# Into the MLP: order of the late operand sums, where the upper squares are summed, and which engine splits the last output weights

## The chip, the cores and the metric

One core of a Trainium2 chip runs the whole program in one launch. The metric is the time on the device in microseconds (us). All numbers are 32-bit floats. TensorE multiplies, VectorE and ScalarE and GpSimd work element by element, and the queues that SyncE issues move data to and from device memory.

## The reference, cut to what matters

Two layers of a decoder trunk on 1040 tokens (16 learned ones and 1024 given ones) of width 1024. Layer 0 mixes by a short convolution and a gated delta rule, layer 1 by windowed attention; each layer then has a gated MLP. What lies around the change is the end of each mixer and the beginning of each MLP:

```python
h = h + mix                                  # mix = heads @ w_out (or wo)
hn = h * rsqrt(mean(h*h, -1) + EPS) * w      # rms_norm, per token
gate, val = split(hn @ w_up, 2)              # 1024 -> 2 x 2816
gate = causal_dwconv(gate, conv_w)           # width 3
h = h + (silu(gate) * val) @ w_down
```

## The kernel before, in words

Activations stand with the model dimension on the 128 partitions: `h` is eight tiles `h[0]` to `h[7]` of 128 by 1040 tokens. Each product of full precision is made of three reduced ones: every operand x is split into a high part (a cast by ScalarE) and a low part (x minus the high part, by VectorE, or by GpSimd in `load_w`), and TensorE adds high*high, high*low and low*high.

The up projection (`ffn`) takes its product of a 2 by 2 block matrix (weights: gate and value, lower and upper half of the model dimension; tokens: lower and upper half, `tk[0]` and `tk[1]`, of 520 tokens each in layer 0 and 516 in layer 1) with seven block products instead of eight. There are 22 columns of blocks i, and each makes products 0 to 6. Their token operands are X[0] to X[6], made once per layer by `parts` (L747): X[0] and X[1] are the lower tokens of either half of the model dimension times the norm's weight, X[2] and X[3] are sums of blocks (L783 to L788), X[4], X[5] and X[6] are the late ones: sums by L792 and L795, and one plain block. Each X[j] has four tiles k, and each tile costs one cast on ScalarE and one subtraction on VectorE (L751, or L754 with the norm's weight). The weights' operands are sums as well: `w1` is the gate's weights themselves, `w2` is split from `sa` (L869, L870), `w3` and `w4` from `sb` (L879, L887) and a raw block, each split by `wsplit` (L809 cast, L810 low part).

The products run in two accumulators of PSUM, `A` and `C`, of two buffers each. In block i, `A` holds products 0, 2, 4 and 5 one after the other, and ScalarE copies it out between them (`snap`, L826: `p1` after product 0, `u2` after product 2, `u3` after product 4); product 1 has a `C` of its own, and products 3 and 6 share one. So product 4 can't start before the copy `u2` is made. The first product of block i+1 is issued inside block i.

The norm's factor is one number per token, so it is applied late, on the results (L896). Its making stands between the early and the late operands in the program: for each half s of the tokens, ScalarE squares `h[k]` (L737, L740), VectorE adds the eight squares into `ss[s]` (L741), TensorE sums over the partitions with a matrix of ones (L760, into a `C`), and a chain of steps between ScalarE (L763, L764, L766) and VectorE (L767, L768, twice) makes the inverse root. Both halves share the scratch tiles `sg`, `th` and `u2`, so the second half's chain follows the first's, and the copy `u2` of block 0 follows both.

The order of instructions on an engine is not the order of the text. A planner, run when the program is built, plays the program on a clock of its own and lists for each engine what is ready, in the main the earlier line first; `tc.issue_after(ins)` makes it list every instruction of a block that runs on `ins`'s engine behind `ins`. On the chip each engine keeps that list's order. The tiles of X beyond the first five take the places of the mixer's result tiles, which come free as TensorE reads them for the last time.

The mixer of layer 0 ends with eight output products (L692 to L699, in the order h0, h4, h1, h5, h2, h6, h3, h7). That of layer 1 ends with `outputs(1, yb, QCH[2:])` (L1229): four weights, each loaded by `load_w` (L129; the low part by GpSimd at L135), and for each two short products of the last 346 tokens, added to `h` at L1205.

Of the kernel before, what the change touches and what calls it, by code (L numbers as in the profile page):

```python
# [7 lines left out]
F32 = mybir.dt.float32  # L8
# [3 lines left out]
AF = mybir.ActivationFunctionType  # L12
ALU = mybir.AluOpType
# [5 lines left out]
KT = D // P  # L19
# [63 lines left out]
def trunk(tc, hT0, w_in, w_ab, w_out, w_q, w_k, w_v, w_o, w_up, w_down, vec, cst, out):  # L83
# [3 lines left out]
    with ctx:  # L87
# [40 lines left out]

        def load_w(src, nk, name):  # L129
            raw = wp.tile([P, nk, P], F32, tag="wraw", name=name + "r")  # L130
            sp.dma_start(raw, src)
            hi = wp.tile([P, nk, P], F32R, tag="whi", name=name + "h")
            lo = wp.tile([P, nk, P], F32R, tag="wlo", name=name + "l")
            ac.copy(hi, raw)  # L134
            gp.tensor_tensor(lo, raw, hi.bitcast(F32), ALU.subtract)  # L135
            return hi, lo
# [569 lines left out]
        def ffn(h, layer, last):  # L706
# [10 lines left out]
            with tc.tile_pool(name=f"fx{layer}", bufs=5, side="right", reuse_waits="tile") as xb:  # L717
                with tc.tile_pool(name=f"f{layer}", bufs=1, reuse_waits="tile") as fp, \
# [11 lines left out]

                    sums = full("r", 2)
                    ss = [sums[:, s * hf:s * hf + hf] for s in range(2)]
                    for j, k in enumerate((0, 4, 1, 5, 2, 6, 3, 7)):
                        sp.dma_start(hd[k][:, o0:], h[k][:, o0:])
                        for s in range(2):
                            if j == 0:
                                ac.activation(ss[s], h[k][:, tk[s]], AF.Square)  # L737
                            else:
                                sq = half("p1", 1, "sq") if s else half("u3", 1, "sq")
                                ac.activation(sq, h[k][:, tk[s]], AF.Square)  # L740
                                ve.tensor_tensor(ss[s], ss[s], sq, ALU.add)  # L741

                    X = [[None] * 4 for _ in range(7)]

                    def parts(j, k, src, vcol=None):
# [3 lines left out]
                        if vcol is None:  # L749
                            ac.copy(hi, src)  # L750
                            ve.tensor_tensor(lo, src, hi.bitcast(F32), ALU.subtract)  # L751
                        else:
                            ac.activation(hi, src, AF.Copy, scale=vcol)
                            ve.scalar_tensor_tensor(lo, src, vcol, hi.bitcast(F32), ALU.mult, ALU.subtract)  # L754
                        X[j][k] = (hi, lo)

                    def scales(s):
                        ps = wide("C")
                        for b in range(2):
                            pe.matmul(ps[:, b, :q], ones, ss[s][:, b * q:b * q + q], start=True, stop=True)  # L760
                        a, t = (x[:, :hf] for x in (full("sg"), full("th")))
# [25 lines left out]
                    for k in range(4):  # L787
                        parts(3, k, B(0, k, 0))  # L788
                    for s in range(2):
                        scales(s)  # L790
                    for k in range(4):
                        ve.scalar_tensor_tensor(B(0, k, 1), B(1, k, 1), w[4 + k], B(0, k, 1), ALU.mult, ALU.subtract)  # L792
                        parts(4, k, B(0, k, 1))
                    for k in range(4):
                        ve.scalar_tensor_tensor(B(1, k, 0), B(1, k, 0), w[4 + k], t2[k], ALU.mult, ALU.subtract)  # L795
                        parts(5, k, B(1, k, 0))
                        parts(6, k, B(1, k, 1), w[4 + k])

# [60 lines left out]
                    for i in range(NF):  # L859
# [8 lines left out]
                        sa = fp.tile([P, KT, P], F32, tag="ws", name="sa", bufs=2)  # L868
                        ve.tensor_tensor(sa[:, 4:8], v1, v2, ALU.add)  # L869
                        ve.tensor_tensor(sa[:, 0:4], sa[:, 4:8], g1, ALU.subtract)  # L870
                        w2 = wtile()
                        wsplit(w2, 0, KT, sa)
                        product(A, w2, 0, 2, False)
# [4 lines left out]
                        sb = fp.tile([P, KT, P], F32, tag="ws", name="sb", bufs=2)  # L878
                        ve.tensor_tensor(sb[:, 0:4], g1, v1, ALU.subtract)  # L879
                        w3 = wtile()  # L880
                        wsplit(w3, 0, 4, sb[:, 0:4])
                        wsplit(w3, 4, 4, v2)
                        product(A, w3, 0, 4, False)
                        u3 = snap("u3", A)
                        v = full("v")
                        ve.tensor_tensor(two(v[:, hf:2 * hf]), two(u3), C[:, :, :q], ALU.subtract)  # L886
                        ve.tensor_tensor(sb[:, 4:8], sa[:, 0:4], g2, ALU.subtract)  # L887
                        if i + 1 < NF:
# [3 lines left out]
                        w4 = wtile()  # L892
                        wsplit(w4, 0, 4, sb[:, 4:8])
                        product(C, w4, 0, 6, False)
# [42 lines left out]
        def swa(h, sqp):  # L937
# [5 lines left out]
            with tc.tile_pool(name="l1", bufs=1, reuse_waits="tile") as lp:  # L943
# [248 lines left out]

                def outputs(G, ys, cs, pairs=range(4)):
                    for i in pairs:
                        w = load_w(w_o[i, G], 8, "wo")
                        for j in range(2):
# [31 lines left out]
                parts(1, yb, QCH[2:])  # L1228
                outputs(1, yb, QCH[2:])  # L1229
            return ho[0::2] + ho[1::2]  # L1230
# [80 lines left out]
```

## Time and profile before

| | |
|---|---|
| median of 3 runs | 2427.57 us (2425.96 to 2429.2) |
| the profiled execution: its own time | 2428.64 us |
| the profiled execution: span from the first to the last instruction | 2426.9 us |
| TensorE matmul, busy | 2345.5 us, 97% |
| VectorE, busy | 1656.2 us, 68% |
| ScalarE, busy | 981.6 us, 40% |
| GpSimd, busy | 483.6 us, 20% |
| mean granted TensorE clock | 0.989 of full speed |

The span holds the mixer of layer 0 up to 583.7 us, its MLP up to about 1296 us, the mixer of layer 1 up to 1709.5 us and its MLP to the end. PE is TensorE's matmul, PEld its weight load, DVE is VectorE, ACT is ScalarE, POOL is GpSimd and SP is SyncE. In a timeline the matmuls overlap, so a matmul's cost to the stream is the distance to the start of the next one.

### The profile page before, as it was taken

The page shows a single profiled execution, that of the slowest core. Times are in us where ns is not written, and L with a number is a line of the kernel's source. Part 1 is how long each engine was busy: PE and PEld are TensorE (multiplying, and loading weights), DVE is VectorE, ACT ScalarE, POOL GpSimd, SP SyncE. Part 2 cuts the span into 40 slices and gives each one's busy share as a digit, 9 for nine tenths or more (in the row PEclk, how much of TensorE's full clock was granted, in tenths as well). Part 3 has the DMA queues.
Part 4 walks back from the last instruction along what each step waited for, and adds up shares of the span by engine and source line. Part 5 has one row for each costly group of instructions (what it writes and reads, how often), then busy time and mean ns, then how long its engine had stood idle before and what let it go on. Part 6 is the DMA issues. An engine that isn't in the chain of part 4 may idle for free.

```text
span 2426.9 us, 40063 instructions
## 1 busy us (share of the span) xinstructions
PE 2345.5 (97%) x16060; PEld 2214.8 (91%) x16060; DVE 1656.2 (68%) x2836; ACT 981.6 (40%) x1980; POOL 483.6 (20%) x421
## 2 busy tenths in 40 slices
PE   8999999999899999999999999999699999999999
PEld 7989999998899999999999987878699999998887
DVE  8886735667677777785536578778877777778432
ACT  6445213435344444432225456645544444433110
POOL 1113323520000000012225245454000000002221
PEclk9999999999999999999999999999899999999999
DMA  3234434141122222253212100202222222234222
GB/s 136 93 111 133 162 120 142 58 167 71 71 79 79 80 79 79 76 194 114 85 61 106 44 27 19 96 18 82 93 79 79 83 81 80 81 140 159 86 66 100
DMA packets 93481, 224.83 MB, mean 93 GB/s; under 512 B 18672, under 2 KB 30264, under 8 KB 93296
## 3 DMA queue, kind: packets, MB, share of 16 engines
q1 hardware_dynamic: 93296, 222.28, 26.7%
q8 instruction: 126, 2.06, 0.3%
q14 instruction: 59, 0.48, 0.1%
HBM read 166.08 MB, written 56.15 MB: 92 GB/s over the span
## 4 chain that ended last, share of the span: by engine, by line
PE 82%; DVE 12%; ACT 4%; issue 1%; DMA 1%; POOL 0%; SPq 0%; ACTq 0%; DVEq 0%; POOLq 0%
PE mm L147 38%; PE A L820 20%; PE C L820 15%; PE po L1020 1%; DVE qt L251 1%; PE scp L1074 1%; DVE yl L171 1%; ACT sc L1092 1%; DVE X L751 1%; PE qkp L973 0%; ACT xh L182 0%; PE po L1143 0%; DVE Xd L499 0%; DVE wlo L810 0%; DVE fq L497 0%
## 5 line engine op out<-in xcount | busy, mean ns | idle before, releaser
L820 PE MATMUL A<-X,whi 128*128 128x260 f32 (+1 forms) x2816 | 515.3, 284 | 16.4 <-ACT u L826 15.8
L147 PE MATMUL mm<-y,wdh 128*128 128x346 f32 (+2 forms) x1760 | 471.1, 350 | 1.6 <-DVE r L895 1.6
L820 PEld LDWEIGHTS A<-X,whi 128*128 128x128 f32 x2816 | 436.1, 190 | 17.9 <-ACT u L826 17.0
L820 PE MATMUL C<-X,whi 128*128 128x260 f32 (+1 forms) x2112 | 391.5, 284 | 7.7 <-DVE v L886 5.9
L820 PE MATMUL A<-X,wlo 128*128 128x260 f32 (+1 forms) x1408 | 394.2, 283 | 0.0
L135 POOL TENSOR_TENSOR wdl<-wdr,wdh 128x512 fp32r<-128x512 f32 (+1 forms) x80 | 117.8, 1473 | 1301.4 <-ACT wdh L134 1297.0
L147 PEld LDWEIGHTS mm<-y,wdh 128*128 128x128 f32 x1760 | 315.1, 188 | 32.8 <-DVE r L895 2.1
L820 PEld LDWEIGHTS C<-X,whi 128*128 128x128 f32 x2112 | 329.2, 190 | 8.6 <-DVE v L886 6.3
L147 PE MATMUL mm<-y,wdl 128*128 128x346 f32 (+2 forms) x880 | 307.4, 350 | 0.0
L820 PE MATMUL C<-X,wlo 128*128 128x260 f32 (+1 forms) x1056 | 297.2, 283 | 0.0
L820 PEld LDWEIGHTS A<-X,wlo 128*128 128x128 f32 x1408 | 265.6, 190 | 0.0
L931 DVE TENSOR_TENSOR h<-mm,h 128x346 f32<-128x346 f32 (+2 forms) x200 | 115.9, 583 | 208.0 <-PE mm L147 207.5
L820 PEld LDWEIGHTS C<-X,wlo 128*128 128x128 f32 x1056 | 200.0, 190 | 0.0
L147 PEld LDWEIGHTS mm<-y,wdl 128*128 128x128 f32 x880 | 165.5, 188 | 15.4
L810 DVE TENSOR_TENSOR wlo<-sa,whi 128x1024 fp32r<-128x1024 f32 x44 | 53.9, 1225 | 171.4 <-ACT whi L809 171.4
L134 ACT CAST wdh<-wdr 128x512 fp32r<-128x512 f32 (+1 forms) x80 | 53.1, 664 | 265.5 <-PE mm L147 221.1
L809 ACT CAST whi<-sb 128x512 fp32r<-128x512 f32 x88 | 54.6, 621 | 130.2 <-PE C L820 128.4
L147 PE MATMUL mm<-xl,wqkvh 128*128 128x346 f32 (+1 forms) x288 | 96.0, 333 | 1.3 <-DVE xl L183 1.3
L826 ACT COPY u<-A 128x520 f32<-128x520 f32 (+1 forms) x88 | 52.1, 592 | 111.4 <-PE A L820 108.3
L147 PE MATMUL mm<-xh,wqkvh 128*128 128x346 f32 (+1 forms) x288 | 96.2, 337 | 0.7 <-DVE row L269 0.7
L809 ACT CAST whi<-sa 128x1024 fp32r<-128x1024 f32 x44 | 46.1, 1048 | 120.4 <-PE A L820 120.4
L147 PE MATMUL mm<-xh,wqkvl 128*128 128x346 f32 (+1 forms) x288 | 93.3, 326 | 0.0
(401 smaller groups left out, 5259.1 us busy)
## 6 DMA issues: line engine op xcount, KB each, us to landing
wg<-in_w_up SPq DMA_DIRECT2D x44, 512.0 KB, 3.4
wv<-in_w_up SPq DMA_DIRECT2D x44, 512.0 KB, 3.4
wdr<-in_w_down SPq DMA_DIRECT2D x48, 256.0 KB, 2.6
fy<-sg SPq DMA_DIRECT2D x22, 520.0 KB, 2.6
yf<-fy SPq DMA_DIRECT2D x22, 520.0 KB, 4.9
fy<-sg SPq DMA_DIRECT2D x22, 516.0 KB, 2.6
yf<-fy SPq DMA_DIRECT2D x22, 516.0 KB, 4.7
wdr<-in_w_down SPq DMA_DIRECT2D x32, 320.0 KB, 3.0
```

Source lines behind the costliest of these rows:

```text
L134: ac.copy(hi, raw)
L135: gp.tensor_tensor(lo, raw, hi.bitcast(F32), ALU.subtract)
L147: pe.matmul(ps[:, :n], a[:, j, :], b[:, c0:c0 + n], start=(i == 0), stop=(i == last))
L171: ve.tensor_tensor(dst_l, src, dst_h.bitcast(F32), ALU.subtract)
L251: ve.scalar_tensor_tensor(d, buf[:, pad + c0 - i:pad + c0 - i + n], taps[W - 1 - i], tmp[:, :n], ALU.mult, ALU.add)
L751: ve.tensor_tensor(lo, src, hi.bitcast(F32), ALU.subtract)
L809: ac.copy(hi, src)
L810: ve.tensor_tensor(lo, src, hi.bitcast(F32), ALU.subtract)
L820: pe.matmul(ps[:, b, :q], a[:, at + k, :], x[:, c], start=(start and n == 0), stop=(n == 11), skip_group_check=not start)
L826: ac.copy(two(t), ps[:, :, :q])
L931: ve.tensor_tensor(hn[m][:, s], ps[:, :n], hn[m][:, s], ALU.add)
L1020: pe.matmul(ps, a, b, start=(start and j == 0), stop=(stop and j == 2))
```

## The change

There are four edits.

1. The squares of the upper tokens (s = 1) are no longer added by VectorE. TensorE multiplies each by the matrix of ones and adds them in a `C` named `upper`, taken at the beginning of `ffn`; each square is two matmuls more, and the upper half's own pair after the sum goes. The squares use the tiles `u2` and `p1` in turn.
2. The late operand sums (L792, L795) and the low parts of X[4], X[5] and X[6] are listed on VectorE behind `half_x`, the low part of the last tile of X[3].
3. The weight sums and splits of `w2` in block 1, and of `w3` and `w4` in blocks 0 and 1, are listed on VectorE behind `half_x` as well; the sum `sb[:, 4:8]` stands some lines earlier.
4. In layer 1's last output products, the weights' low part is made by VectorE and not by GpSimd.

```diff
-        def load_w(src, nk, name):
+        def load_w(src, nk, name, eng=gp):
...
-            gp.tensor_tensor(lo, raw, hi.bitcast(F32), ALU.subtract)
+            eng.tensor_tensor(lo, raw, hi.bitcast(F32), ALU.subtract)
...
-                    sums = full("r", 2)
-                    ss = [sums[:, s * hf:s * hf + hf] for s in range(2)]
+                    ss = full("r", 2)[:, :hf]
+
+                    upper = wide("C")
                     for j, k in enumerate((0, 4, 1, 5, 2, 6, 3, 7)):
                         sp.dma_start(hd[k][:, o0:], h[k][:, o0:])
-                        for s in range(2):
-                            if j == 0:
-                                ac.activation(ss[s], h[k][:, tk[s]], AF.Square)
-                            else:
-                                sq = half("p1", 1, "sq") if s else half("u3", 1, "sq")
-                                ac.activation(sq, h[k][:, tk[s]], AF.Square)
-                                ve.tensor_tensor(ss[s], ss[s], sq, ALU.add)
+                        if j == 0:
+                            ac.activation(ss, h[k][:, tk[0]], AF.Square)
+                        else:
+                            sq = half("u3", 1, "sq")
+                            ac.activation(sq, h[k][:, tk[0]], AF.Square)
+                            ve.tensor_tensor(ss, ss, sq, ALU.add)
+                        sq = half("u2" if j % 2 else "p1", 1, "sq")
+                        ac.activation(sq, h[k][:, tk[1]], AF.Square)
+                        for b in range(2):
+                            pe.matmul(upper[:, b, :q], ones, sq[:, b * q:b * q + q], start=(j == 0), stop=(j == 7))
...
                             ac.copy(hi, src)
-                            ve.tensor_tensor(lo, src, hi.bitcast(F32), ALU.subtract)
+                            last_lo[:] = [ve.tensor_tensor(lo, src, hi.bitcast(F32), ALU.subtract).ins]
...
                     def scales(s):
-                        ps = wide("C")
-                        for b in range(2):
-                            pe.matmul(ps[:, b, :q], ones, ss[s][:, b * q:b * q + q], start=True, stop=True)
+                        ps = upper
+                        if s == 0:
+                            ps = wide("C")
+                            for b in range(2):
+                                pe.matmul(ps[:, b, :q], ones, ss[:, b * q:b * q + q], start=True, stop=True)
...
                         parts(3, k, B(0, k, 0))
+
+                    half_x = last_lo[0]
                     for s in range(2):
                         scales(s)
-                    for k in range(4):
...
+                    with tc.issue_after(half_x):
+                        for k in range(4):
+                            ve.scalar_tensor_tensor(B(0, k, 1), B(1, k, 1), w[4 + k], B(0, k, 1), ALU.mult, ALU.subtract)
+                            parts(4, k, B(0, k, 1))
+                        for k in range(4):
+                            ve.scalar_tensor_tensor(B(1, k, 0), B(1, k, 0), w[4 + k], t2[k], ALU.mult, ALU.subtract)
+                            parts(5, k, B(1, k, 0))
+                            parts(6, k, B(1, k, 1), w[4 + k])
...
-                        ve.tensor_tensor(sa[:, 4:8], v1, v2, ALU.add)
-                        ve.tensor_tensor(sa[:, 0:4], sa[:, 4:8], g1, ALU.subtract)
                         w2 = wtile()
-                        wsplit(w2, 0, KT, sa)
+                        with tc.issue_after(half_x) if i == 1 else nullcontext():
+                            ve.tensor_tensor(sa[:, 4:8], v1, v2, ALU.add)
+                            ve.tensor_tensor(sa[:, 0:4], sa[:, 4:8], g1, ALU.subtract)
+                            wsplit(w2, 0, KT, sa)
...
-                        ve.tensor_tensor(sb[:, 0:4], g1, v1, ALU.subtract)
                         w3 = wtile()
-                        wsplit(w3, 0, 4, sb[:, 0:4])
-                        wsplit(w3, 4, 4, v2)
+                        with tc.issue_after(half_x) if i < 2 else nullcontext():
+                            ve.tensor_tensor(sb[:, 0:4], g1, v1, ALU.subtract)
+                            ve.tensor_tensor(sb[:, 4:8], sa[:, 0:4], g2, ALU.subtract)
+                            wsplit(w3, 0, 4, sb[:, 0:4])
+                            wsplit(w3, 4, 4, v2)
...
-                        ve.tensor_tensor(sb[:, 4:8], sa[:, 0:4], g2, ALU.subtract)
...
-                            wsplit(w4, 0, 4, sb[:, 4:8])
+                        with tc.issue_after(half_x) if i < 2 else nullcontext():
+                            wsplit(w4, 0, 4, sb[:, 4:8])
...
-                outputs(1, yb, QCH[2:])
+                outputs(1, yb, QCH[2:], eng=ve)
```

## Rows read from the trace of the kernel before

**Rows 1.** Busy time, share of the span and instructions of each engine (page).
```profile
PE 2345.5 (97%) x16060; PEld 2214.8 (91%) x16060; DVE 1656.2 (68%) x2836; ACT 981.6 (40%) x1980; POOL 483.6 (20%) x421
```

**Rows 2.** Stretches: length; busy (count) of PE, PEld, DVE, ACT, POOL; clock; DMA.
```profile
503.28:580.26 76.98, 76.98 (x484) 76.98 (x485) 44.06 (x58) 21.67 (x31) 14.36 (x6) 1.00 0.39 149
583.74:614.84 31.10, 20.10 (x154) 19.06 (x153) 29.62 (x48) 21.49 (x36) 0.00 (x0) 0.97 0.14 52
614.84:620.30 5.46, 5.45 (x24) 5.24 (x24) 0.00 (x0) 0.00 (x0) 0.00 (x0) 0.53 0.01 3
1689.54:1745.42 55.88, 36.75 (x227) 35.04 (x225) 54.57 (x82) 33.66 (x54) 5.31 (x2) 0.83 0.40 142
```

**Rows 3.** Chain that ended last, both entries: start, length, what.
```profile
613.40 0.71 DVE rstd L768
...
614.84 5.47 PE A L820 x24
...
1744.72 0.71 DVE rstd L768
...
1746.15 4.77 PE A L820 x24
```

**Rows 4.** Waits, 1680 to 1747 us: engine and line <- releaser: sum, times, longest.
```profile
PE C L760 <- DVE r L741: 7.9, 1, 7.9
...
PE A L820 <- ACT u L826: 7.2, 1, 7.2
PE mm L147 <- DVE h L1205: 6.5, 4, 2.8
PEld mm L147 <- issue: 5.5, 3, 3.1
```

**Rows 5.** Timeline of DVE, entry of layer 0: start, length, instruction.
```profile
562.11 2.90 DVE L792 SCALAR_TENSOR_TENSOR h<-h,vt,h 128x520 f32<-128x520 f32 x1
...
568.29 0.68 DVE L879 TENSOR_TENSOR sb<-wg,wv 128x512 f32<-128x512 f32 x1
...
589.76 0.69 DVE L741 TENSOR_TENSOR r<-r,sq 128x520 f32<-128x520 f32 x1
590.37 0.68 DVE L869 TENSOR_TENSOR sa<-wv 128x512 f32<-128x512 f32 x1
590.97 0.75 DVE L795 SCALAR_TENSOR_TENSOR h<-h,vt,v 128x520 f32<-128x520 f32 x1
591.64 0.69 DVE L767 TENSOR_TENSOR th<-sg,th 128x520 f32<-128x520 f32 x1
...
595.90 1.30 DVE L751 TENSOR_TENSOR X<-h,X 128x520 fp32r<-128x520 f32 x2
```

**Rows 6.** Timeline of DVE, entry of layer 1.
```profile
1692.79 2.47 DVE L741 TENSOR_TENSOR r<-r,sq 128x516 f32<-128x516 f32 x1 [0.57 <-ACT sq L740]
...
1695.61 0.68 DVE L741 TENSOR_TENSOR r<-r,sq 128x516 f32<-128x516 f32 x1
...
1698.58 2.86 DVE L792 SCALAR_TENSOR_TENSOR h<-h,vt,h 128x516 f32<-128x516 f32 x1
...
1719.85 0.69 DVE L767 TENSOR_TENSOR th<-sg,th 128x516 f32<-128x516 f32 x1
1720.45 0.69 DVE L741 TENSOR_TENSOR r<-r,sq 128x516 f32<-128x516 f32 x1
```

**Rows 7.** GpSimd's timeline there, and VectorE's split of 128x1024 (groups by form).
```profile
1692.30 2.40 POOL L135 TENSOR_TENSOR wol<-wor,woh 128x1024 fp32r<-128x1024 f32 x1 [2.77 <-ACT woh L134]
1697.97 2.91 POOL L135 TENSOR_TENSOR wol<-wor,woh 128x1024 fp32r<-128x1024 f32 x1 [3.27 <-PE mm L147]
...
L810 DVE TENSOR_TENSOR wlo<-sa,whi 128x1024 fp32r<-128x1024 f32 x44 | 53.9, 1225 | 171.4 <-ACT whi L809 171.4
```

**Rows 8.** Timeline of PE at the end of layer 0's mixer.
```profile
583.91 1.11 PE L760 MATMUL C<-r,ct 128*128 128x260 f32 x4 [0.17 <-DVE r L741]
584.67 0.59 PE L820 MATMUL A<-X,whi 128*128 128x260 f32 x2
```

More of the change, by code (lines that the diff above doesn't have):

```diff
@@ L1 @@
 import numpy as np
-from contextlib import ExitStack
+from contextlib import ExitStack, nullcontext
 import concourse.bass as bass
@@ L729, in full @@
                         return fp.tile([P, 2 + 2 * hf], F32, tag=tag, name=tag, bufs=bufs)
-                    sums = full("r", 2)
-                    ss = [sums[:, s * hf:s * hf + hf] for s in range(2)]
+                    ss = full("r", 2)[:, :hf]
+                    upper = wide("C")
                     for j, k in enumerate((0, 4, 1, 5, 2, 6, 3, 7)):
                         sp.dma_start(hd[k][:, o0:], h[k][:, o0:])
-                        for s in range(2):
-                            if j == 0:
-                                ac.activation(ss[s], h[k][:, tk[s]], AF.Square)
-                            else:
-                                sq = half("p1", 1, "sq") if s else half("u3", 1, "sq")
-                                ac.activation(sq, h[k][:, tk[s]], AF.Square)
-                                ve.tensor_tensor(ss[s], ss[s], sq, ALU.add)
+                        if j == 0:
[8 more added lines that the diff above has]
+                            pe.matmul(upper[:, b, :q], ones, sq[:, b * q:b * q + q], start=(j == 0), stop=(j == 7))
                     X = [[None] * 4 for _ in range(7)]
+                    last_lo = []
                     def parts(j, k, src, vcol=None):
@@ L788, in ffn @@
                         parts(3, k, B(0, k, 0))
+                    half_x = last_lo[0]
                     for s in range(2):
                         scales(s)
-                    for k in range(4):
[L792 to L797, printed above, removed]
+                    with tc.issue_after(half_x):
[6 more added lines that the diff above has]
+                            parts(6, k, B(1, k, 1), w[4 + k])
                     nw = [0]
@@ L1191, in parts, with outputs @@
                             split(ys[t][0][:, sl], ys[t][1][:, sl], qg[G][t][:, sl])
-                def outputs(G, ys, cs, pairs=range(4)):
+                def outputs(G, ys, cs, pairs=range(4), eng=gp):
                     for i in pairs:
-                        w = load_w(w_o[i, G], 8, "wo")
+                        w = load_w(w_o[i, G], 8, "wo", eng)
                         for j in range(2):
```

## The prediction

> **What bounds the kernel now.** The page first: TensorE is busy 97% of the span and VectorE 68% [rows 1], so only places where TensorE waits are worth anything. The stretches show two. At the end of layer 0's mixer TensorE has no hole at all (76.98 us busy of 76.98); then, entering the MLP, it is busy 20.1 us of 31.1 while VectorE is busy 29.6 of them. Entering layer 1's MLP it is 36.8 us of 55.9 against VectorE's 54.6, and the granted clock falls to 0.83 [rows 2]. So in both entries VectorE sets the pace. The chain says which of its work ends last: the second half's inverse root (L768, ending at 614.11 and at 1745.43 us), then the copy `u2`, then product 4 of block 0 [rows 3]. That product waits 7.2 us for the copy in layer 1, and before that product 1 stands 7.9 us behind the ones-matmuls that wait for the last sum of upper squares [rows 4]. Product 4 of layer 0, after its wait, runs at 0.53 of the clock, the lower of the two levels: 5.45 us for 24 matmuls [rows 2]. Until it, TensorE can do only products 0 to 3 of block 0 and 0 and 1 of block 1: the rest needs X[4] or a weight tile that is still in use. The time of an entry is therefore the time at which product 4 starts (with its four needs: X[4], the first half of `w3`, `u2`, and so the chain), plus what is put on TensorE before it.
>
> The order of VectorE is a plan's, and the diff changes only its rules. I count work that stands ahead of the chain's end before, and say what leaves and enters.
>
> **Prices.** A sum of 520 tokens costs VectorE 0.61 us (from L741 at 589.76 to the next start), a weight sum or split of 512 columns 0.60, a scaled sum (L792, L795, L754) 0.67 (590.97 to 591.64) [rows 5]; in layer 1 the same to 0.01. A split of 1024 columns costs 1.2 us [rows 7]. A pair of ones-matmuls holds TensorE 0.76 us, from 583.91 to the next matmul at 584.67 [rows 8].
>
> **Edit 1 in layer 0.** Of VectorE's seven additions for the upper tokens only the last (0.61 us, at 589.76) stands in the full stretch; the others stood where VectorE was busy 44 us of 77 [rows 2, 5] and are worth nothing. On TensorE eight pairs come. Seven squares are ready before the mixer's last matmul: 7 x 0.76 = 5.3 us, and with no hole in TensorE there, what is issued there costs in full. The plan could also hold them back into the entry, where TensorE waits anyway: 0. I take 5.3, the end that the full row shows. The eighth pair replaces the pair that goes.
>
> A rule of the Trainium skill weighs against this edit: "FP8 and Floating Point Precision", section "TensorE Precision Notes", has a true 32-bit product pass the array four times. By it a pair of 260 columns takes an estimated 2 x 4 x 260 / 2.4 GHz = 0.87 us, and seven pairs 6.1 us instead of 5.3, so that the gain below would be 0.8 us smaller. The trace shows 0.76 us [rows 8]; I go by that.
>
> **Edits 2 and 3 in layer 0.** What enters the full stretch: three L792 and one L795 that VectorE did before 580 us in idle time (the last L792 at 562.11), 4 x 0.67 = 2.7 us, and the two sums and two splits of `w3` of block 0, done from 568.29 on, 4 x 0.60 = 2.4 us [rows 5]. What can leave from ahead of the chain's end: the addition above, 0.6; block 1's two sums for `w2` (the first at 590.37), its two for `w3`, two splits and its L866, 7 x 0.60 = 4.2; the split of `w4`, 0.6. Sum: 2.7 + 2.4 - 0.6 - 4.2 - 0.6 = -0.3 us, if all of X[5] and X[6] still stands ahead of product 4. That is 4 x (0.67 + 0.61 + 0.67) = 7.8 us, which product 4 doesn't need. X[3] ends at about 597 us now [rows 5]; the chain begins at 591.64, in the middle of the early sums, and its eight steps take 22.5 us, 2.8 each, since each queues behind some four others. With the late work behind `half_x` the chain, which is the earlier text, should get ahead of part of it. If half of the 7.8 us goes behind, the sum is -4.2. I take the middle, -2.2; the bounds are -8.1 (all of it behind) and +4.5 (nothing leaves but the one addition). Layer 0: 5.3 - 2.2 = +3.1 us.
>
> **Edits 1 and 4 in layer 1.** Here VectorE is full from 1689.5 us on [rows 2], so all seven additions count (1695.61 to 1720.45): 7 x 0.61 = 4.3 us off [rows 6]. While GpSimd splits an output weight, a VectorE instruction on it takes far longer: L741 2.47 us instead of 0.68 beside the split at 1692.30, L792 2.86 instead of 0.75 beside that at 1697.97 [rows 5 to 7]. These 1.8 + 2.1 us go; two splits of 1.2 us come to VectorE. Net -5.8 us. (The other two splits lie before 1689.5, in the same trade; I count nothing.) What is queued behind the new splits on VectorE are the additions to `h` (L1205), for which TensorE waits now 6.5 us; their stalls go, so I expect no new wait. The pairs of ones-matmuls, 7 x 0.76 = 5.3 us, lie beside these 6.5 us and the 5.5 us before weights [rows 4]: cost 0, and 5.3 if the cover is gone.
>
> **Edits 2 and 3 in layer 1.** Nothing enters: the late sums (L792 at 1698.58) and `w3` already stand in the full stretch, ahead of X[3]. Block 1's seven can leave, -4.2: together -10.0. Half of X[5] and X[6] behind product 4 gives -13.9. I take -12; bounds -5.8 (nothing but the removals) and -17.8 (all of it).
>
> **Sum.** +3.1 - 12 = -8.9 us against the profiled execution's 2428.64 us (its span is 2426.9, and 1.7 lie around it): 2419.7. The median of the runs is 1.07 us below that execution, so 2418.7; I say 2418.5. What is late next: VectorE's low parts of X[5] and X[6], then nothing, since from product 5 on TensorE has no wait now. That `upper` holds one of the two `C` buffers from the beginning costs nothing: before, the second half's sum held the same buffer up to the same step.
>
> **The rivals.** (a) *The chain gets clear of the late work altogether and the squares fill TensorE's waits*: layer 0 -8.1, layer 1 -17.8, 2428.64 - 25.9 - 1.1 = 2401.6. For it: the chain is earlier in the text. Against it: it was so before, and each step still queued behind some four instructions. (b) *Only the removals pay*, and the order of product 4's needs doesn't improve: layer 0 5.3 - 0.3, layer 1 -5.8: -0.8, 2426.7. For it: VectorE's total in layer 0 is the same to 0.3 us. (c) *The late work takes the wait's place*: all of it comes in one block right behind `half_x`, VectorE's list stays full to the end, and the chain's last step still stands at the end of a list that has become longer. Layer 0: +4.5 + 5.3 = 9.8; layer 1: -5.8 + 5.3 = -0.5; together +9.3, 2436.8. It decides from the point where layer 0's loss exceeds layer 1's gain, so where product 4 of layer 0 starts over 31.1 us after the mixer's last matmul and layer 1 gains less than 10. For it: in layer 0 idle time of VectorE is given up for full time. Against it: layer 1, with the longer wait, gives none up. That a plan with other rules might not put the work where the diff wants it is in (b) and (c).
>
> **How the numbers follow.** The forecast 0.52 (its own range 2411 to 2425), (a) 0.14, (b) 0.19, (c) 0.15. A difference under 0.2%, 4.9 us, can't be told from no change here. Faster by more, under 2422.7: nine tenths of the forecast and (a), 0.61, with a little of (b): 0.62. Within: the rest of the forecast and most of (b): 0.20. Slower: (c) and the rest of (b): 0.18. The range 2404 to 2432 leaves out the far half of (a) and the greater part of (c).
>
> **What would show it.** Product 4 of block 0 in layer 0 starts about 29 us after the mixer's last matmul (31.1 now), in layer 1 some 12 us earlier than now against the start of its mixer's last output products (1746.15 now); VectorE has seven L741 a layer, none over 1 us in layer 1's entry; the stretch before layer 0's entry is some 5 us longer. Wrong would be: the first L795 ahead of L751 of X[3], product 4 of layer 0 later than 31.1 us after the mixer, squares' matmuls that wait and hold products behind them on TensorE, or an output product of layer 1 waiting for its split on VectorE.

## The result, and the profile after

The changed kernel is slower: 2440.48 us (median; 2438.74 to 2442.29 in 4 runs) against 2426.98 us before, a ratio of 1.0054 with a 95% interval of 1.0042 to 1.0067. The prediction of 2418.5 us was wrong in sign, and the time lies outside its range.

In the new file the lines are shifted: the chain's steps L763, L764, L766, L767, L768 are now L770, L771, L773, L774, L775; the in-place scaling of `h[k]`'s upper half (L783) is L790, and the sums that follow it (L784, L785) L791 and L792; the late sums L792 and L795 are L802 and L805; the low parts L751 are L756; `wsplit`'s low part is L820, a product L830, `snap` L836, the first sum into `r` L876. New are L743 (ScalarE's squares of upper tokens) and L745 (their ones-matmuls); L767 is now the lower half's pair, L760 before.

The page's busy line, against [rows 1]. TensorE works 15 us more, VectorE 16 us less, and the span is 12 us longer:

```profile
PE 2360.8 (97%) x16116; PEld 2229.2 (91%) x16116; DVE 1639.9 (67%) x2826; ACT 983.6 (40%) x1980; POOL 473.6 (19%) x417
```

Stretches of the changed kernel, in the columns of [rows 2]: the same 77 us of layer 0's mixer; the entry from the mixer's last matmul to product 4; product 4; then layer 1's last output products and its entry up to product 4.

```profile
503.28:580.26 76.98, 76.98 (x486) 76.98 (x485) 24.04 (x37) 16.58 (x24) 13.87 (x6) 1.00 0.35 133
582.72:627.63 44.91, 29.30 (x183) 27.44 (x181) 38.57 (x60) 28.42 (x45) 0.00 (x0) 0.83 0.16 54
627.63:633.16 5.53, 5.52 (x24) 5.26 (x24) 0.00 (x0) 0.00 (x0) 0.00 (x0) 0.52 0.11 44
...
1681.08:1712.29 31.21, 29.14 (x173) 28.66 (x172) 26.12 (x46) 17.68 (x28) 0.00 (x0) 0.95 0.62 219
1712.29:1757.02 44.73, 29.43 (x181) 27.61 (x180) 38.43 (x59) 27.79 (x45) 0.00 (x0) 0.84 0.15 54
```

The mixer is still without a hole (it ends 0.9 us earlier, but its first addition to `h`, L699, was already 0.8 us earlier), and VectorE does only 24.0 us of work beside it instead of 44.1. Some 9.5 us of that are six additions, which are gone; some 10 us are late sums and block 0's `w3`, which edits 2 and 3 moved into the entry; 2.6 us are L784 and L785. Groups of VectorE in these 77 us, with busy time and mean ns of one, the first two before, the third after:

```profile
L741 DVE TENSOR_TENSOR r<-r,sq 128x520 f32<-128x520 f32 x12 | 13.7, 1143 | 6.6 <-ACT sq L740 6.6
L792 DVE SCALAR_TENSOR_TENSOR h<-h,vt,h 128x520 f32<-128x520 f32 x3 | 6.6, 2188 | 0.0
...
L741 DVE TENSOR_TENSOR r<-r,sq 128x520 f32<-128x520 f32 x6 | 4.2, 700 | 4.5 <-ACT sq L740 4.5
```

The entry takes 44.9 us to product 4, where it was 31.1. VectorE isn't even full there any more (38.6 of 44.9 us; before it was 29.6 of 31.1), so this entry waits for a sequence and not for an engine's total.

Timeline of VectorE and, in the second fence, of ScalarE, entry of layer 0 of the changed kernel; the bracket is the idle time before and what ended it:

```profile
587.47 0.70 DVE L756 TENSOR_TENSOR X<-t,X 128x520 fp32r<-128x520 f32 x1 [0.69 <-ACT X L755]
589.53 0.76 DVE L791 SCALAR_TENSOR_TENSOR h<-h,vt 128x520 f32<-128x520 f32 x1 [1.36 <-ACT h L790]
...
593.68 0.76 DVE L791 SCALAR_TENSOR_TENSOR h<-h,vt 128x520 f32<-128x520 f32 x1 [1.21 <-ACT h L790]
...
597.52 2.53 DVE L756 TENSOR_TENSOR X<-h,X 128x520 fp32r<-128x520 f32 x4
599.97 2.77 DVE L802 SCALAR_TENSOR_TENSOR h<-h,vt,h 128x520 f32<-128x520 f32 x4
...
607.74 0.70 DVE L774 TENSOR_TENSOR th<-sg,th 128x520 f32<-128x520 f32 x1
...
626.20 0.70 DVE L775 SCALAR_TENSOR_TENSOR rstd<-th,rs_y 128x520 f32<-128x520 f32 x1
```

```profile
588.10 0.64 ACT L743 ACTIVATE sq<-h 128x520 f32<-128x520 f32 x1 [0.66 <-PE C L745]
588.77 0.73 ACT L790 ACTIVATE h<-h,vt 128x520 f32<-128x520 f32 x1
...
592.25 0.64 ACT L743 ACTIVATE sq<-h 128x520 f32<-128x520 f32 x1 [0.51 <-PE C L745]
592.92 0.73 ACT L790 ACTIVATE h<-h,vt 128x520 f32<-128x520 f32 x1
...
599.53 0.64 ACT L773 ACTIVATE th<-rs_y 128x520 f32<-128x520 f32 x1
```

Two things are to be seen. First, squares (L743) wait for ones-matmuls (L745), the in-place scaling L790 of a tile stands behind its square, and VectorE waits for L790: before, VectorE waited for no scaling (L783) in the entry. Second, the chain's `th` is ready at 600.17, but its first step on VectorE (L774) starts at 607.74, behind the eight late sums, L876, two weight sums and a split. The chain ends at 626.91 us (614.11 before, [rows 3]).

TensorE's timeline there. The first ones-matmuls stand right behind the mixer's last matmul, and the C that holds them is not free before the second half's chain begins (L770):

```profile
582.56 0.32 PE L147 MATMUL mm<-yh,woutl 128*128 128x346 f32 x1
582.72 1.92 PE L745 MATMUL C<-sq,ct 128*128 128x260 f32 x8
...
606.17 0.77 PE L830 MATMUL C<-X,whi 128*128 128x260 f32 x2 [3.33 <-DVE r L876]
618.47 0.80 PE L830 MATMUL C<-X,whi 128*128 128x260 f32 x2 [7.87 <-ACT sg L770]
627.63 0.80 PE L830 MATMUL A<-X,whi 128*128 128x260 f32 x2 [4.12 <-ACT u L836]
```

Layer 1 repeats it; these are its waits from 1681 to 1764 us, in the columns of [rows 4]. The 6.5 us of output products waiting for L1205 have become 2.1, but product 1 of block 1, product 4 and product 3 wait 7.6, 4.0 and 3.3 us:

```profile
PE C L830 <- ACT sg L770: 7.6, 1, 7.6
...
PE A L830 <- ACT u L836: 4.7, 2, 4.0
...
DVE h L791 <- ACT h L790: 3.6, 4, 1.9
...
PE C L830 <- DVE r L876: 3.3, 1, 3.3
...
PE mm L147 <- DVE h L1218: 2.1, 1, 2.1
```

What answers to [rows 6] and [rows 7] is as forecast: groups of VectorE in layer 1's tail and entry, with the shortest, median and longest of one (ns). The additions are all short, and the splits take the 1.2 us of any split.

```profile
L741 DVE TENSOR_TENSOR r<-r,sq x7: 686/697/703, 1682.5 to 1699.7; 128x516 f32<-128x516 f32 x7
...
L135 DVE TENSOR_TENSOR wol<-wor,woh x4: 1221/1226/1231, 1688.7 to 1704.2; 128x1024 fp32r<-128x1024 f32 x4
```

### The profile page after: what moved, and what is told of

The parts are those of the page before. It is cut to its first block, busy times and chain, and to the rows that moved or that the text cites. A ratio compares the mean times of both kernels' runs of the same rounds, so it can differ in the third digit from the quotient of the medians.

```text
span 2439.0 us, 40170 instructions
## 1 busy us (share of the span) xinstructions
PE 2360.8 (97%) x16116; PEld 2229.2 (91%) x16116; DVE 1639.9 (67%) x2826; ACT 983.6 (40%) x1980; POOL 473.6 (19%) x417
## 4 chain that ended last, share of the span: by engine, by line
PE 82%; DVE 12%; ACT 4%; DMA 1%; issue 1%; POOL 0%; SPq 0%; ACTq 0%; DVEq 0%; POOLq 0%
PE mm L147 38%; PE A L830 20%; PE C L830 15%; PE po L1033 1%; DVE qt L251 1%; PE scp L1087 1%; DVE yl L171 1%; DVE X L756 1%; ACT sc L1105 1%; ACT xh L182 1%; PE qkp L986 0%; DVE Xd L499 0%; PE C L745 0%; DVE fq L497 0%; DVE wlo L820 0%
## 5 line engine op out<-in xcount | busy, mean ns | idle before, releaser
L830 PE MATMUL A<-X,whi 128*128 128x260 f32 (+1 forms) x2816 | 516.8, 285 | 10.8 <-ACT u L836 10.8
L830 PEld LDWEIGHTS A<-X,whi 128*128 128x128 f32 x2816 | 436.8, 190 | 12.6 <-ACT u L836 12.2
L830 PE MATMUL C<-X,whi 128*128 128x260 f32 (+1 forms) x2112 | 398.8, 287 | 28.0 <-ACT sg L770 15.5
L830 PE MATMUL A<-X,wlo 128*128 128x260 f32 (+1 forms) x1408 | 395.0, 284 | 0.6 <-DVE wlo L820 0.6
L830 PEld LDWEIGHTS C<-X,whi 128*128 128x128 f32 x2112 | 334.9, 193 | 29.3 <-ACT sg L770 15.9
L830 PE MATMUL C<-X,wlo 128*128 128x260 f32 (+1 forms) x1056 | 300.3, 286 | 0.0
L830 PEld LDWEIGHTS A<-X,wlo 128*128 128x128 f32 x1408 | 266.0, 190 | 1.1 <-DVE wlo L820 1.0
L830 PEld LDWEIGHTS C<-X,wlo 128*128 128x128 f32 x1056 | 203.1, 193 | 0.1
L820 DVE TENSOR_TENSOR wlo<-sa,whi 128x1024 fp32r<-128x1024 f32 x44 | 53.9, 1226 | 172.8 <-ACT whi L819 172.8
L836 ACT COPY u<-A 128x520 f32<-128x520 f32 (+1 forms) x88 | 52.1, 592 | 112.9 <-PE A L830 109.2
```

What stands on the lines that cost most here:

```text
L830: pe.matmul(ps[:, b, :q], a[:, at + k, :], x[:, c], start=(start and n == 0), stop=(n == 11), skip_group_check=not start)
L836: ac.copy(two(t), ps[:, :, :q])
```

## The experiments

Three theories. **Theory 1**: edit 1 makes the loss, since its ones-matmuls are listed behind the mixer, only two tiles hold squares, and `h[k]` is scaled in place after its square; so the sums for X[2] and X[3] move into the entry. **Theory 2**: edits 2 and 3 make it, since the late block stands ahead of the chain. **Theory 3**: edit 4 is what layer 1 gains.

The experiments' kernels were timed in 5 to 11 runs each, in four groups on different chips, each group beside runs of the kernel before (medians 2427.0 to 2428.4 us); the changed kernel has its 4 runs. The ratios are to those runs. The last two columns come from the profiled executions, as differences to before: the start of the run of 48 matmuls on A that holds block 1's product 4 and block 2's product 0, by which the entry's waits are over. In layer 0 it is counted from the start of the span (632.6 us before), in layer 1 from the first of the mixer's last output products (92.6 us before).

| kernel | median us | ratio, 95% interval | layer 0 | layer 1 |
|---|---|---|---|---|
| after | 2440.5 | 1.0054 (1.0042 to 1.0067) | +12.9 | +1.2 |
| e1: without edit 1 | 2426.0 | 0.9994 (0.9985 to 1.0003) | +6.3 | -7.4 |
| e2: edit 1 alone | 2433.4 | 1.0029 (1.0020 to 1.0038) | +4.8 | -4.2 |
| e3: edit 4 alone | 2423.7 | 0.9981 (0.9972 to 0.9991) | -0.2 | -4.7 |
| e4: after, eight square tiles | 2423.6 | 0.9983 (0.9974 to 0.9992) | +3.1 | -4.7 |
| e5: e1, late work behind the chain | 2414.6 | 0.9952 (0.9939 to 0.9965) | -2.5 | -12.2 |
| e6: e4, late work behind the chain | 2412.3 | 0.9943 (0.9931 to 0.9955) | -2.5 | -14.5 |
| e7: e4 without edits 2 and 3 | 2420.2 | 0.9969 (0.9957 to 0.9981) | -1.0 | -6.8 |
| e8: edits 2, 3 in layer 1 only, and 4 | 2423.0 | 0.9978 (0.9968 to 0.9988) | -0.7 | -5.7 |
| e9: after, late work behind the chain | 2429.3 | 1.0007 (0.9998 to 1.0016) | +9.5 | -5.9 |
| e10: e6, only unneeded work late | 2412.4 | 0.9936 (0.9923 to 0.9948) | -7.0 | -11.4 |
| e11: e10 without edit 1 | 2412.1 | 0.9935 (0.9923 to 0.9948) | -5.6 | -11.9 |
| e12: layer 0 as e10, layer 1 as e6 | 2408.8 | 0.9926 (0.9912 to 0.9939) | -6.6 | -12.4 |

The two columns' sum agrees with the difference of the medians within 3 us, but for e2, whose profiled execution (2430.7 us) lies 2.7 under its median.

Each column comes from one execution. That of layer 0 also holds what stood ahead of the entry: the mixer's last matmul started at 583.4 us before, at 580.0 in e6, 581.4 in e10, 581.9 in e12, 584.0 in e11 and 584.5 in e7 (the others within 1.0 us of before), and these shifts were there at the mixer's first addition to `h` (L699). Whether they are scatter or come of the edits, no run tells. In layer 1, e1 and e8 have the same text and differ by 1.7 us.

**e1, without edit 1.** The squares go back to VectorE:

```diff
-                        sq = half("u2" if j % 2 else "p1", 1, "sq")
-                        ac.activation(sq, h[k][:, tk[1]], AF.Square)
-                        for b in range(2):
-                            pe.matmul(upper[:, b, :q], ones, sq[:, b * q:b * q + q], ...)
+                                sq = half("p1", 1, "sq") if s else half("u3", 1, "sq")
+                                ac.activation(sq, h[k][:, tk[s]], AF.Square)
+                                ve.tensor_tensor(ss[s], ss[s], sq, ALU.add)
```

Expected:

> Edits 2, 3 and 4 stay; the upper tokens' squares are added by VectorE again, as before. Theory 1 (edit 1 makes the loss: with two square tiles the upper squares wait for ones-matmuls that are listed behind the mixer, and the sums for X[2] and X[3], which need h[k]'s upper half scaled in place after its square, move into the entry): product 4 of block 0 in layer 0 starts about 30 us after the mixer's last matmul instead of 44.8, VectorE has no wait on ScalarE's L790 there, and the time is about 2417 us (2412 to 2424). Theory 2 (edits 2 and 3 make it: the late block right behind half_x stands ahead of the chain): product 4 still starts over 38 us after the mixer, and the time is 2431 us or more.

Between the two: 2426.0 us, product 4 37.5 us after the mixer. The stall is gone, the late block is not. VectorE of e1 (L752 is X[3]'s low parts, L796 the first late sums, L768 the chain's first step, L769 its last), and ScalarE's step that makes `th` ready for it:

```profile
588.74 2.52 DVE L752 TENSOR_TENSOR X<-h,X 128x520 fp32r<-128x520 f32 x4
591.18 2.77 DVE L796 SCALAR_TENSOR_TENSOR h<-h,vt,h 128x520 f32<-128x520 f32 x4
...
598.37 0.69 DVE L768 TENSOR_TENSOR th<-sg,th 128x520 f32<-128x520 f32 x1
...
619.58 0.70 DVE L769 SCALAR_TENSOR_TENSOR rstd<-th,rs_y 128x520 f32<-128x520 f32 x1
```

```profile
590.24 0.64 ACT L767 ACTIVATE th<-rs_y 128x520 f32<-128x520 f32 x1
```

X[3] is ready at 591.3 us. Before, its four low parts stood among nine of `h` from 592.86 to 599.65 us, which the trace doesn't tell apart, so it was ready at 596.6 us at the earliest: 5 us or more were gained. The chain's `th` is ready at 590.88 us, but its first step starts at 598.37, 6.7 us later than before (591.64, [rows 5]): the early operands were bought with the chain.

**e2, edit 1 alone.** Edits 2, 3 and 4 of the changed kernel are undone (as the first line, at all four places; the sum `sb[:, 4:8]` goes back to its old place):

```diff
-                    with tc.issue_after(half_x):
+                    with nullcontext():
...
-                outputs(1, yb, QCH[2:], eng=ve)
+                outputs(1, yb, QCH[2:])
```

Expected:

> The kernel before with edit 1 alone (upper tokens' squares summed by TensorE); the late sums and the weight splits are listed as before, and GpSimd splits the last output weights. Theory 1: layer 0's product 4 starts 40 us or more after the mixer, layer 1's entry is longer by some 5 us too, and the time is 2438 to 2448 us, about 15 us over before. Theory 2: edit 1 costs at most the eight pairs of ones-matmuls, 5.3 us a layer at the utmost against 4.3 us of additions that go: 2425 to 2431 us.

Again between: +6.4 us, product 4 37.3 us after the mixer (31.1 before). So neither theory carries the loss alone.

**e3, edit 4 alone**, on the kernel before:

```diff
-                outputs(1, yb, QCH[2:])
+                outputs(1, yb, QCH[2:], eng=ve)
```

Expected:

> The kernel before with edit 4 alone (VectorE and not GpSimd splits layer 1's last four output weights). Theory 3 (this is where layer 1 gains: the output products no longer wait, and VectorE's additions beside the splits are short): 8 to 10 us faster than before, about 2418 us, with the wait of TensorE for L1205 and for weights in the mixer's tail mostly gone and the entry as long as before. Rival: the earlier end of the mixer's tail only lengthens the wait for the chain, since VectorE's work to the end of the chain is what counts: 4 us at most, 2423 to 2427 us.

The time, 2423.7 us, is in the rival's range. Stretches before and in e3, each from the first of the last output products to the mixer's end and from there to product 4:

```profile
1670.59:1709.51 38.92, 32.44 (x173) 31.39 (x172) 35.74 (x53) 20.66 (x32) 10.12 (x4) 0.87 0.47 166
1709.51:1746.15 36.64, 21.51 (x154) 20.57 (x152) 35.17 (x57) 22.85 (x38) 0.00 (x0) 0.82 0.23 83
```

```profile
1670.47:1698.09 27.62, 27.58 (x173) 27.10 (x172) 25.39 (x46) 16.36 (x26) 0.00 (x0) 1.00 0.59 204
1698.09:1740.59 42.50, 21.27 (x154) 20.38 (x152) 41.77 (x67) 27.20 (x45) 0.00 (x0) 0.78 0.25 85
```

TensorE's waits in the tail are all gone (27.58 of 27.62 us busy): 11.3 us. VectorE then works 41.8 of 42.5 us, and 5.9 us go back: it paces both stretches, and only what VectorE itself saves counts.

**e4, a tile for each upper square.** All edits stay:

```diff
+                    spare = [full("sg"), full("th"), full("r", 2)]
+                    spare = [x[:, e * hf:e * hf + hf] for x in spare for e in range(2)]
...
-                        sq = half("u2" if j % 2 else "p1", 1, "sq")
+                        sq = spare[j - 2] if j > 1 else half("u2" if j % 2 else "p1", 1, "sq")
```

Expected:

> The kernel after with a tile of its own for each of the eight upper squares (halves of sg, th and the second r, which are free then, beside p1 and u2), so that no square waits for a ones-matmul; the ones-matmuls still stand behind the mixer's last matmul, all edits stay. Theory 1: the squares, L790 and the sums for X[2] and X[3] go back into the mixer's tail; product 4 of layer 0 starts at most 34 us after the mixer, and the time is 2416 to 2427 us, at least 13 us below after. Theory 2: the late block still stands ahead of the chain, product 4 starts over 38 us after the mixer, 2434 us or more.

2423.6 us: the tiles alone take back 16.9 us, more than the 13.5 that were lost, as theory 1 has it. ScalarE of e4 (L745 squares, L792 scaling) does this work in the mixer again, and only the eight pairs (L747) stand behind it. (Why the plan lists them there, with the first square ready at 504.8 us, no run tells.) In VectorE's timeline X[3]'s low parts (L758) end at 589.9 us instead of 600.0; the last line is product 4's start (L832):

```profile
549.32 0.63 ACT L745 ACTIVATE th<-h 128x520 f32<-128x520 f32 x1
551.75 0.73 ACT L792 ACTIVATE h<-h,vt 128x520 f32<-128x520 f32 x1 [1.79 <-DMA fh<-h]
```

```profile
582.64 1.91 PE L747 MATMUL C<-sq,ct 128*128 128x260 f32 x8
...
587.90 1.92 PE L747 MATMUL C<-r,ct 128*128 128x260 f32 x8
589.65 1.04 PE L769 MATMUL C<-r,ct 128*128 128x260 f32 x4
```

```profile
587.41 2.52 DVE L758 TENSOR_TENSOR X<-h,X 128x520 fp32r<-128x520 f32 x4
...
618.75 0.52 PE L832 MATMUL A<-X,whi 128*128 128x260 f32 x2 [4.62 <-ACT u L838]
```

Product 4 starts at 618.75, 36.0 us after the mixer, later than the 34 expected: theory 2's part is still there.

**e5 and e6, the late work behind the chain's last step** (e5 on e1, e6 on e4):

```diff
-                            ve.scalar_tensor_tensor(rstd[:, tk[s]] if i else y, t, m3, y, ALU.add, ALU.mult)
+                            steps.append(ve.scalar_tensor_tensor(rstd[:, tk[s]] if i else y, t, m3, y, ALU.add, ALU.mult).ins)
...
+                    half_x = steps[7]
                     with tc.issue_after(half_x):
```

(`steps` holds the chain's eight instructions on VectorE; the seventh index is the last.) Expected:

> Edits 2, 3 and 4 without edit 1 (as in e1), but the late sums and splits are listed behind the last step of the second half's inverse root instead of behind half_x, so that no late work stands ahead of the chain. Theory 2 (in layer 0 the late block takes 7 us ahead of the chain's first step, and product 4 waits for the chain): the chain of layer 0 ends by 606 us instead of 620.3, product 4 then waits for X[4] and w3 instead of u2 and starts between 609 and 616 us (621.0 in e1), and the time is 5 to 12 us under e1: 2414 to 2421 us. If the block's place is not what costs, the work ahead of product 4 is the same either way, product 4 starts at 620 us or later, and the time stays at 2424 us or more.

> All four edits with a tile for each upper square (as in e4), and the late work behind the chain's last step. Theories 1 and 2 together: both waits are gone, product 4 of layer 0 starts under 614 us (618.8 in e4), 2412 to 2420 us. If the squares' pairs (32 matmuls, 7.2 us in e4 between the mixer's last matmul and product 0) now decide, because TensorE and not VectorE is late, the time stays at that of e4, 2422 to 2426 us.

Both as theory 2 says: 11.4 us under e1, 11.3 under e4. In e6 the chain of layer 0 ends at 600.6 us (626.9 in after; L777 below is its last step). What is late next are the other needs of product 4, X[4] and `w3`, now behind the late sums; it starts piecemeal, as TensorE's lines of e6 show (L833 is a product, L758 the low parts of X, L823 that of `wsplit`):

```profile
599.89 0.70 DVE L777 SCALAR_TENSOR_TENSOR rstd<-th,rs_y 128x520 f32<-128x520 f32 x1
...
608.42 0.58 PE L833 MATMUL A<-X,whi 128*128 128x260 f32 x1 [0.78 <-DVE X L758]
612.67 0.58 PE L833 MATMUL A<-X,wlo 128*128 128x260 f32 x1 [3.67 <-DVE wlo L823]
```

**e7 and e8.** e7 is e4 with edits 2 and 3 undone as in e2; e8 is e1 with them in layer 1 alone (`last` is true there), at all four places (the sum `sb[:, 4:8]` stays in its new place in both layers):

```diff
-                    with tc.issue_after(half_x):
+                    with tc.issue_after(half_x) if last else nullcontext():
```

Expected:

> Edits 1 and 4 with a tile for each upper square, edits 2 and 3 undone (the late sums stand where the plan puts them, as before). Theory 2: layer 0 is 3 to 6 us shorter than in e4, since VectorE has seven additions less and the late sums are done in the mixer's idle time again: product 5 of layer 0 at 618 to 621 us (624.1 in e4, 621.0 before), 2417 to 2422 us. Rival (edit 1 has a cost of its own on TensorE even without the stall: 7.2 us of pairs ahead of product 0): product 5 not before 624 us, 2423 us or more.

> Edits 2 and 3 in layer 1 alone, edit 4, no edit 1: the places where the runs so far show a gain. Theory 2 says that the late block costs only where it stood in the mixer's idle time before (layer 0) and gains in layer 1, where VectorE was full anyway: from the distance between layer 1's last output products and product 5 (81.0 us before, 76.3 with edit 4 alone, 73.6 in e1) 7.4 us under before, 2417 to 2421 us. Rival: e1's gain in layer 1 came with its later start there, and the time is that of edit 4 alone, 2423 to 2425 us.

e7 came out as theory 2 said: product 5 at 620.0 us, 2420.2 us. e8 missed: with 2423.0 us it can't be told from edit 4 alone, and the 2.7 us that e1 showed beyond e3 in layer 1 were not found again. The late block behind `half_x` is worth nothing that is shown in layer 1 either.

**e9, the stall alone.** The kernel after, with its two square tiles, and e5's diff. Expected:

> The kernel after, all four edits and its two square tiles, but with the late work behind the chain's last step (as in e5 and e6). Theory 1: the stalled squares still hold the sums for X[2] and X[3] in the entry (VectorE waits for L790 there), X[3] ends some 8 us later than in e6 (587.4 us), the chain starts as much later, and product 5 of layer 0 starts 5 to 9 us later than in e6 (618.5): 2419 to 2428 us against e6's 2412.3. If the stall costs only together with the late block: product 5 within 3 us of e6, 2411 to 2416 us.

Theory 1, and by more than expected in time: 2429.3 us. Product 5 is at 629.0 us, 10.5 later than in e6, but 3.3 of these are e6's earlier mixer; from the mixer's end they are 7.2, as expected, and layer 1 has another 8.6. VectorE of e9 waits for L790 exactly as in after:

```profile
590.21 0.76 DVE L791 SCALAR_TENSOR_TENSOR h<-h,vt 128x520 f32<-128x520 f32 x1 [1.35 <-ACT h L790]
...
594.36 0.76 DVE L791 SCALAR_TENSOR_TENSOR h<-h,vt 128x520 f32<-128x520 f32 x1 [1.21 <-ACT h L790]
...
601.25 0.69 DVE L774 TENSOR_TENSOR th<-sg,th 128x520 f32<-128x520 f32 x1
```

With e4, e6 and e9 there is a square of four kernels with all edits. Medians in us:

| | late work behind `half_x` | behind the chain |
|---|---|---|
| two square tiles | 2440.5 (after) | 2429.3 (e9) |
| eight square tiles | 2423.6 (e4) | 2412.3 (e6) |

The stall costs 16.9 or 17.0, the late block's place 11.2 or 11.3. By the ratios, which take each group's own runs of before, it is 17 or 16 and 11 or 10; each ratio has an interval of 2 to 3 us to either side, so the two add up within the noise. Together they are 28 us: the 13.5 that were lost, and the 15 by which e6 is under before.

**e10, e11 and e12, what product 4 needs first.** In e10 X[4]'s sums and block 0's `w3` leave the late work; e11 is the same without edit 1; e12 does it in layer 0 alone:

```diff
-                    with tc.issue_after(half_x):
+                    with tc.issue_after(half_x) if last else nullcontext():
                         for k in range(4):
                             ve.scalar_tensor_tensor(B(0, k, 1), B(1, k, 1), w[4 + k], B(0, k, 1), ALU.mult, ALU.subtract)
                             parts(4, k, B(0, k, 1))
+                    with tc.issue_after(half_x):
                         for k in range(4):
...
-                        with tc.issue_after(half_x) if i < 2 else nullcontext():
+                        with tc.issue_after(half_x) if i == 1 or last and i == 0 else nullcontext():
```

Expected:

> As e6 (all four edits, a tile for each upper square, late work behind the chain's last step), but only what product 4 doesn't need is late: X[5], X[6], block 1's weight work and w4. X[4]'s sums and block 0's w3 are free for the plan again and go into the mixer's idle time. In e6 product 4 waited 3.7 us in layer 0 and 3.9 us in layer 1 for w3's split behind the late sums, besides the 1.8 to 2.2 us and 0.8 us before it. Theory 2 (what stands on VectorE ahead of product 4's needs is what an entry costs): these waits go, product 4 starts right behind TensorE's own six products, at 604 to 609 us, and the time is 6 to 12 us under e6: 2400 to 2406 us. If VectorE's total up to there is what counts, product 4 gains under 2 us a layer: 2408 us or more.

> As e10 but without edit 1 (the upper squares are added by VectorE). Edit 1's pairs cost TensorE 7.2 us ahead of product 0 in layer 0 and in layer 1 (e6), its seven additions 4.3 us of VectorE. If TensorE is late in an entry once the waits are gone, e11 is 2 to 8 us faster than e10 (product 0 starts at 584.4 instead of 587.9); if VectorE still is, 2 to 8 us slower, as e5 was to e6 in layer 1.

> Layer 0 as e10 (X[4]'s sums and block 0's w3 free, only what product 4 doesn't need is late), layer 1 as e6 (all late work behind the chain's last step). Reason: counted to the first 48 matmuls of block 1's products 4 and 5, e10 was 4.5 us ahead of e6 in layer 0 (VectorE has idle time in the mixer there) and 3.0 us behind it in layer 1 (VectorE has none). If each entry is decided by what VectorE had free before it, the two gains add: 3 to 5 us under e6, 2407 to 2410 us. If the entries act on each other, the time stays at 2412 us.

e10 did at product 4 what was expected (605.67 us, no wait), but the time stayed at e6's: later products of layer 0 now wait for X[5] (1.55 us at the longest), so that layer 0 gains 4.5 us over e6 (6.0 from the mixer's end), and layer 1, where VectorE had no idle time to take X[4]'s sums, loses 3.1. e11 shows no difference to e10, where 2 to 8 us either way were expected: with tiles enough, edit 1 is a trade of TensorE's time for VectorE's without a net that can be measured. e12 came in the expected range, at 2408.8 us the fastest by its median: 0.9926 of before, where the changed kernel is at 1.0054. (The intervals of e6, e10 and e11 overlap with its own.) Its layer 1 shows only 1.0 of the 3.1 us over e10 in the profiled executions, so that the reason given for the last 3.5 us is not fully borne out. (The 48 matmuls that its expectation speaks of are block 1's product 4 and block 2's product 0.) Its stretch from layer 0's mixer to product 4 has no hole and the full clock:

```profile
582.17:606.12 23.95, 23.95 (x171) 22.90 (x171) 21.34 (x35) 17.98 (x30) 0.00 (x0) 1.00 0.06 24
```

## Why the prediction was wrong

**What bounds the kernel.** Right in the main: the loss is where product 4 starts, and what VectorE does before it decides that; e5 and e6 gain 11 us by VectorE's order alone. But it is the order and the waits, not VectorE's total: in after VectorE is idle for 6 us of the entry. And product 4's start isn't all of it: in e10 product 4 waits for nothing, later products wait for X[5], and the time is e6's.

**Edit 1 in layer 0, the first step that failed.** It was given +5.3 us, for pairs issued in the mixer's full stretch, or 0 for pairs held back into the entry. They were held back: all eight pairs stand behind the mixer's last matmul, and the mixer's stretch is not 5 us longer. But being held back was not free. The step asked what the pairs cost TensorE, and not who waits for the tiles that they read. With two tiles, the third upper square waits for the first pair; the scaling in place (L783 before) waits for that square; three of the four L784 and L785 of before, and the low parts of X[2] and X[3] with them, wait for the scaling. Before, all four L784 and three L785 were done in VectorE's idle time in the mixer, and the low parts stood in the entry without a wait for a scaling. In the profiled executions this stall costs layer 0 9.8 us (after against e4) and layer 1 5.9 us; in the time, 17 us. The two tiles were there to be read: six of eight squares had no tile until TensorE came. It is not the amount of work that costs: with tiles enough (e4) VectorE does 27.9 us beside the mixer, only 3.9 more than in after. It is the sequence, with X[3], and `half_x` with it, 10 us later (600.0 against 589.9).

The price of a pair was also low. In a row of pairs one takes 0.876 us ((589.65 - 582.64) / 8, in e4), and not 0.76, which was read where a shorter matmul follows [rows 8]. The estimate from the Trainium skill, "FP8 and Floating Point Precision", section "TensorE Precision Notes", of 0.87 us agrees with that, and the row that was set against it was not a pair's full price: in e4 too the last pair, with product 0 behind it, shows 0.69 us (589.65 to 590.34).

**Edits 2 and 3 in layer 0, the second step that failed.** -2.2 us were taken, with bounds of -8.1 and +4.5; e1 shows +6.3 (with edit 4, which does nothing in layer 0: e3, -0.2). The bounds counted how much work stands ahead of the chain's end, but not that the chain's first step itself could be put back behind a block. That "the chain, which is the earlier text, should get ahead of part of it" was an assumption about the plan, and the list shows the opposite: in e1 a block of 7.2 us (the eight late sums, two weight sums and a split) stands ahead of the chain's first step, whose operand was ready before it. Why the plan puts it there stays open. Where the chain does come first (e5), product 5 is 8.7 us earlier than in e1.

**Layer 1, the third.** The removals came out nearly as summed: e7, which has edits 1 and 4 without the stall and without the late block, shows -6.8 us, and 5.8 were worked out. But the terms were not right one by one: edit 4's share was 1.8 + 2.1 - 2.4 = 1.5 us, and alone it brings 4.7, so that the sum's nearness is in part luck. That TensorE's stalls in the tail mostly go, and no split is waited for, came true. The rest of -12 was the order of the needs, and behind `half_x` it brought nothing that is shown (e8 against e3; e4 even has 2.1 less than e7); the stall then took the removals back: +1.2 in after, -4.7 in e4. With the chain first, layer 1 does show -12.2 and -14.5 (e5, e6).

**The C of `upper`.** That it "costs nothing" was wrong in after, where product 1 of block 1 stands 7.9 us behind L770. It is the late chain that makes it so: in e6 the same C is held from the beginning, and that product waits for nothing.

**The rivals.** (c) named the mechanism of edits 2 and 3, the place (right behind `half_x`) and the point from which it decides; both of its conditions hold. It had 0.15, and 2436.8 us was the nearest of the four times. That it came so near is in part luck: of its 9.8 us in layer 0, 5.3 were for pairs in the mixer's full stretch, which didn't come, and the stall cost 9.8 instead. What it said against itself, that layer 1 gives no idle time up, was no help to layer 1. The stall had no rival of its own. The sign "squares' matmuls that wait and hold products behind them on TensorE" looked at the wrong end: here squares waited for the matmuls.

## What to carry to other kernels

When a sum moves to another engine, follow its source tile, not only its result: who else must wait until that tile has been read, and how many tiles are there until the reader comes? An instruction that writes in place makes the reader's lateness everybody's. And in after, e1, e4, e6 and e9 the work that an order rule put behind a marker came *right* behind the marker: the marker must be the last step of the chain that ends the stage, and what the stage's end itself needs must stay free of the rule.

## What the runs showed of the hardware

A wait can cost more than the wait. After one of 5.86 us, product 4's 24 matmuls took 5.45 us before, at 0.53 of the clock [rows 2], and after one of 4.12 us (and 7.87 a product earlier) 5.53 at 0.52 in after, about the lower of the two levels. In e12, where TensorE was busy without a hole up to it at 1.00, the same product's 24 matmuls took 3.03 us (606.12 to 609.15). But not each wait costs that: in e7 the clock stayed at 1.00 after one of 3.12 us, and the product took 3.13 us, while in e4, after 4.62 us, the product was granted 0.63 on average and took 4.65. Product 4 in e7 and in e4:

```profile
616.17:619.30 3.13, 3.13 (x24) 2.93 (x24) 0.00 (x0) 0.00 (x0) 0.00 (x0) 1.00 0.50 168
```

```profile
618.75:623.40 4.65, 4.65 (x24) 4.46 (x24) 0.00 (x0) 0.00 (x0) 0.00 (x0) 0.63 0.13 53
```
